# Three transformer-like blocks on one core: the two halves of the tokens are set half a stage apart, each half with its own weight tiles

## The chip, the cores and the metric

One Trainium2 chip; the kernel runs on one of its cores. The metric is the device time of one execution in microseconds (us), the median over runs. A core has TensorE (PE in the rows; its weight loads are PEld), VectorE (DVE), ScalarE (ACT), GpSimd (POOL), and SyncE (SP), which issues all DMAs here. Each of these engines takes its instructions in the one order that the built program gives it.

## The reference, cut to what matters

512 tokens of width 1024 go through three blocks in fp32, ten stages in all, in the order f10, m1, f11, f21, m2, f22, m30, f30, m31, f31:

```
f10, f11   x = x + 0.5*(1+gate) * rms_norm(swiglu(modulate(x)))       # D_FF = 2816
m1         spatial gating on 512 channels beside causal attention with forget gates, then w_out
f21, f22   swiglu with norms before and after
m2         RWKV-7 recurrence (chunks of 64) beside a 31-tap convolution, then w_out_2
m30, m31   attention over the 256 keys that an indexer picks (a), beside differential attention (b)
f30, f31   x = x + swiglu(rms_norm(x))
swiglu(h)  = (silu(h @ w_gate) * (h @ w_up)) @ w_down
```

Each stage needs the stage before it for the same tokens. Half 1 of the tokens also needs keys, values or states of half 0 within a mixer (m1, m2, m30, m31); half 0 needs nothing of half 1.

## The kernel before, in words

The 512 tokens are two halves of 256, `hf` 0 and 1. `for ph in phases: for hf in range(2): part(ph, hf)` writes the program down stage by stage. A scheduler then decides each engine's order: every instruction carries a priority, `BASE + (vt[hf] + lag[hf]) * PER_US`, where `vt` counts the matmul time that this half has had so far (`adv`), and `lag[1]` puts half 1 behind half 0 by a number of such us (`LAGS`, set at each stage's `prenorm`). `boost(us)` makes work more urgent by that much: the chains of the mixers have 20 to 80 us of it, loads of weights mostly none (`WB = 0`).

Weights arrive in fp32, as slots of 128x1024 (eight 128x128 tiles). `Weights.slot` loads a slot into one of three staging buffers (`st`), makes an fp16 high part from it on ScalarE and an fp16 low part on VectorE, and puts both into one of the 12 buffers of a ring (`wr`). `three` multiplies high by high, high by low and low by high, so each tile and half costs three matmuls of 256 columns, and a slot 24 of them. `W(name)` gives the one `Weights` of a matrix, so that a slot is loaded and split once, and both halves read it:

```
def W(name):
    if name not in weights:
        weights[name] = Weights(name)
    return weights[name]
```

In an FFN, `gu` holds 44 slots (22 pairs of gate and up, `pgu` in PSUM, evacuated by `fth`, `fac`, `act`) and `dn` 22 slots (`po`). m1 has 28 slots, m2 30, m30 and m31 35 each; 524 in all. In the mixers, `pp`, `pt` and `pgl` are the projections, `ps` the scores of one head (`amx` their maximum, `prob`, `probt`), `pd` and `sc` the indexer's scores, from which `MAX8` and `MATCH_REPLACE8` pick keys, and `pT`, `pA`, `pxy`, `pu`, `psp` belong to the recurrence of m2. Each half has two PSUM buffers for its scores and two for its projections. While f10 runs, the 37.7 MB of `w_ada` also come in and are summed on VectorE (`ada_row`).

Of the kernel before, what the change touches and what calls it, by code (L numbers as in the profile page):

```python
# [44 lines left out]
RB = 80  # L45
SELB = 5
RING = 12
LAGS = {"f10": 26, "m1": 16, "f11": 22, "f21": 26, "m2": 22, "f22": 24,
    "m30": 30, "f30": 22, "m31": 30, "f31": 18}
HOLD = {"m1": -5, "m2": 15, "m30i": 0, "m30b": -5, "m30a": -5, "m31i": 0,  # L50
    "m31b": 0, "m31a": 0}
BASE = 2000000
# [191 lines left out]
def tile_three_blocks(ctx: ExitStack, tc: tile.TileContext, d, col_at, con_at, out, phases=None):  # L244
# [129 lines left out]

    weights = {}

    def W(name):
        if name not in weights:
            weights[name] = Weights(name)
        return weights[name]  # L380

    def three(out_, a, b, first, last, guard):
        (ah, al), (bh, bl) = a, b
# [126 lines left out]
    def ffn(hf, gu, dn, pre, bias, post, key):  # L510
        hh = prenorm(hf, pre, bias, key)
        acts = []
        for n in range(NF):
            adv(hf, 5.23)
            if n % 2 == 0:
                acts.append(m2k(hf, [128, 2, 2, TH], F16, "act"))
            act = acts[-1]
            p = pmm(hf, [128, 2, TH], name="pgu")
            gemm(p[:, 0], W(gu), 16 * n, KD, pair(hh))
            gemm(p[:, 1], W(gu), 16 * n + 8, KD, pair(hh), bank=False)  # L520
            with boost(EB):
                t = t1k(hf, name="fth")
                S.activation(t, p[:, 0], AF.Tanh, scale=0.5 / WS)  # L523
                V.scalar_tensor_tensor(t, t, 1.0, p[:, 0], op0=OP.add, op1=OP.mult)  # L524
                a = t1k(hf, name="fac")
                V.scalar_tensor_tensor(a, t, 0.5 / WS / WS / AS, p[:, 1], op0=OP.mult, op1=OP.mult)  # L526
                split(hf, act[:, 0, n % 2], act[:, 1, n % 2], a)
            beside(key, hf, n)
        x = lambda k: (acts[k // 2][:, 0, k % 2], acts[k // 2][:, 1, k % 2])
        if post is None:  # L530
            out_add(hf, W(dn), NF, x, AS / WS)
            return
        yb = {}

        def y(m):
            if not yb:
                yb[0] = b8k(hf, [128, KD, TH], F32, "y")
            return yb[0][:, m]
        acc = out_tiles(hf, W(dn), NF, x, y, AS / WS, key)
        postnorm(hf, acc, y, post)  # L540


# [15 lines left out]
    def ada_row(g, k, h):  # L558
        src = kv2k(1, name="adw")
        nc.sync.dma_start(out=src, in_=d["w_ada"][g, k, :, h * 512:(h + 1) * 512])  # L560
        if k == 0:
            ada_acc[g, h] = kv2k(0, name="ada")
            V.tensor_scalar(ada_acc[g, h], src, csil[:, 0:1], None, op0=OP.mult)
        else:
            V.scalar_tensor_tensor(ada_acc[g, h], src, csil[:, k:k + 1], ada_acc[g, h], op0=OP.mult, op1=OP.add)  # L565
# [120 lines left out]
    def mixer1(hf):  # L686
# [24 lines left out]
        for j in range(8):  # L711
            adv(hf, 2.6)
            p = pmm(hf, [128, TH], name="pp")
            gemm(p, W("m1_qk"), (j + 4) % 8 * KD, KD, px)
            with boost(MB):
                (kt if j < 4 else qt_).put(j % 4, p, 1.0 / WS if j < 4 else 0.125 / WS)
        m1["k", hf] = kt
# [28 lines left out]
        m1["v", hf] = []  # L746
        for tt in range(2):
            vt_ = kv2k(hf, name="v")
            token_gemm(hf, W("m1_v"), hh, tt, lambda p: S.activation(vt_, p, AF.Copy, scale=1.0 / WS))
            m1["v", hf].append(vt_)  # L750

        now(hf)
# [24 lines left out]
        for j in range(4):  # L777
            adv(hf, 2.6)
            p = pmm(hf, [128, TH], name="pp")
            gemm(p, W("m1_u"), j * KD, KD, px)  # L780
            if j % 2 == 0:
                us.append(m2k(hf, [128, 2, TH], F32, "u"))
            gelu(hf, us[-1][:, j % 2], p)
# [6 lines left out]
        for tt in range(2):  # L790
            g = m2k(hf, name="vg")

            def ev(p, g=g):
                for q in range(2):
                    gelu(hf, g[:, q * 256:(q + 1) * 256], p[:, q * 256:(q + 1) * 256])
            token_gemm(hf, W("m1_g"), hh, tt, ev)
            bn = tiny(hf, 6, "bn")
            V.bn_stats(bn, g)
            mv = tiny(hf, 2, "mv")
# [31 lines left out]
                to_channels(hf, ybs[qt], mix, 4, qt, lambda j: col("gnb", j))  # L831
        ys = [m2k(hf, [128, 2, TH], F32, "ym") for _ in range(4)]
        y = lambda m: ys[m // 2][:, m % 2]
        acc = out_tiles(hf, W("m1_o"), KD, pair(mix), y, 1.0 / WS)
        postnorm(hf, acc, y, one_col(gpost, 8))

    def row_rms(hf, y, n):
# [20 lines left out]
    def mixer2(hf):  # L858
# [36 lines left out]
        for j in order:  # L895
            adv(hf, 2.6)
            p = pmm(hf, [128, TH], name="pp")
            gemm(p, W("m2_s"), j * KD, KD, px)
            with boost(BOOST["m2r"]):
                raw = t1k(hf, name="raw")  # L900
                S.activation(raw, p, AF.Copy, scale=1.0 / WS)
# [17 lines left out]
        def gate_units(j):  # L919
            adv(hf, 5.2)  # L920
            p = pmm(hf, [128, 2, TH], name="pgl")
            gemm(p[:, 0], W("m2_c"), 16 * j, KD, px)
            gemm(p[:, 1], W("m2_c"), 16 * j + 8, KD, px, bank=False)
# [296 lines left out]
        acc = out_tiles(hf, W("m2_o"), KD, lambda k: (mix[:, k, 0], mix[:, k, 1]), y, 1.0 / WS)  # L1220
        postnorm(hf, acc, y, lambda k: col("mpost2", k))


# [3 lines left out]
    def mixer3(hf, l):  # L1227
# [24 lines left out]
        def rotated(w, i0, dst, tab, scale):  # L1252
            adv(hf, 2.6)
            p = pmm(hf, [128, TH], name="pp")
            gemm(p, W(w), i0 * KD, KD, px)
            with boost(RB):
                sw = t1k(hf, name="rsw")
                for b in range(4):
# [80 lines left out]
        vb = []  # L1339
        for tt in range(2):  # L1340
            t = kv2k(hf, name="vb")
            token_gemm(hf, W(f"m3_vb{l}"), hh, tt, lambda p: S.activation(t, p, AF.Copy, scale=1.0 / WS))
            vb.append(t)
        m3["vb", hf] = vb
        now(hf)
# [43 lines left out]
        with boost(BOOST["m3a"]):  # L1389
# [19 lines left out]
        out_add(hf, W(f"m3_o{l}"), KD, pair(mix), 1.0 / WS)  # L1409

# [88 lines left out]
```

## Time and profile before

| | |
|---|---|
| median of 3 runs | 3501.31 us (3500.28 to 3503.44) |
| the profiled execution | 3507.87 us, its span 3506.0 us |
| PE busy | 3309.1 us, 94% |
| PEld busy | 2815.7 us, 80% |
| DVE busy | 2171.3 us, 62% |
| ACT busy | 1545.5 us, 44% |
| mean granted TensorE clock | 0.98 of full speed |
| bytes | 327.89 MB, mean 94 GB/s |

Busy time is the union of an engine's instructions. A matmul's recorded duration reaches past the start of the next one, so that a PE that waits less than the rest of a matmul still counts as busy. In rows of windows a stretch is given from the start of the span, then its length, and for each engine the busy us and the number of instructions.

### The profile page before, as it was taken

To read this page: it belongs to the slowest core of one execution; us is meant where nothing else is said; L and a number is where in the kernel's file an instruction comes from. 1 tells how busy PE (TensorE), PEld (TensorE's weight loads), DVE (VectorE), ACT (ScalarE), POOL (GpSimd) and SP (SyncE) were. 2 spreads that over 40 slices of the span, in tenths; PEclk is the share of its full clock that TensorE was granted. 3 is DMA by queue.
4 is the path that set the end of the run, shared out by engine and by line. 5 is a ranking of instruction groups with operands and counts; after the bars stand their busy time and mean duration, and the time that the engine had idled before them with its cause. 6 is when DMAs were issued, how large, how long until landed. Compare 5 with 4: busy or idle time off the path is not lost. (4 is left out here: it accounts for less than half of the span.)

```text
span 3506.0 us, 71986 instructions
## 1 busy us (share of the span) xinstructions
PE 3309.1 (94%) x30164; PEld 2815.7 (80%) x30164; DVE 2171.3 (62%) x5240; ACT 1545.5 (44%) x3335; POOL 19.1 (1%) x24
## 2 busy tenths in 40 slices
PE   5999999999999999997789999889999998999998
PEld 5888867788888888886678887667888876688887
DVE  8953768844374437688884438887544488855433
ACT  3332466433343324424243326886433278853331
POOL 0000000000000000000000000000000000000000
PEclk9999999999999999987889999999999999999999
DMA  8932313232323332201023323112233321123331
GB/s 276 326 110 91 118 55 130 67 103 97 99 96 102 104 97 91 70 5 34 4 89 104 102 97 99 55 43 67 85 104 102 105 85 51 41 80 109 103 99 47
DMA packets 105591, 327.89 MB, mean 94 GB/s; under 512 B 12584, under 2 KB 18088, under 8 KB 105008
## 3 DMA queue, kind: packets, MB, share of 16 engines
q1 hardware_dynamic: 105264, 323.28, 28.1%
q8 instruction: 236, 3.87, 0.5%
q14 instruction: 91, 0.75, 0.1%
HBM read 321.14 MB, written 2.10 MB: 92 GB/s over the span
## 5 line engine op out<-in xcount | busy, mean ns | idle before, releaser
L314 PEld LDWEIGHTS <-wr 128*128 128x128 f16 x24000 | 2351.0, 99 | 327.8 <-issue 25.5
L314 PE MATMUL pgu<-hh,wr 128*128 128x256 f16 x12672 | 1402.6, 273 | 7.9 <-ACT wr L362 2.3
L363 DVE SCALAR_TENSOR_TENSOR wr<-st,wr 128x1024 f16<-128x1024 f32 x524 | 640.3, 1223 | 353.3 <-ACT wr L362 344.0
L314 PE MATMUL po<-act,wr 128*128 128x256 f16 x6336 | 702.0, 273 | 0.1
L362 ACT ACTIVATE wr<-st 128x1024 f16<-128x1024 f32 x524 | 552.2, 1055 | 323.2 <-PE pgu L314 128.3
L314 PE MATMUL pp<-hh,wr 128*128 128x256 f16 x3072 | 384.1, 274 | 4.8 <-DVE rot L1261 2.2
L523 ACT ACTIVATE fth<-pgu 128x256 f32<-128x256 f32 x264 | 101.3, 384 | 590.4 <-PE pgu L314 590.2
L524 DVE SCALAR_TENSOR_TENSOR fth<-fth,pgu 128x256 f32<-128x256 f32 x264 | 111.0, 420 | 355.9 <-ACT fth L523 355.8
L314 PE MATMUL po<-mix,wr 128*128 128x256 f16 x1536 | 198.0, 282 | 15.9 <-ACT mix L444 9.0
L444 ACT ACTIVATE act<-fac 128x256 f16<-128x256 f32 x264 | 110.2, 417 | 174.1 <-DVE fac L526 173.8
L314 PE MATMUL pt<-wr,hh 128*128 128x512 f16 x576 | 145.4, 383 | 1.6 <-DVE wr L363 1.6
L445 DVE TENSOR_TENSOR act<-fac,act 128x256 f16<-128x256 f32 x264 | 111.3, 422 | 50.5 <-ACT act L444 50.0
L492 DVE TENSOR_TENSOR acc<-acc,sq 128x256 f32<-128x256 f32 x84 | 35.4, 421 | 149.5 <-ACT sq L491 149.5
L1260 ACT ACTIVATE rsw<-pp 32x256 f32<-32x256 f32 x304 | 114.3, 376 | 19.6 <-PE pp L314 15.3
L432 ACT ACTIVATE sq<-x 128x256 f32<-128x256 f32 x154 | 56.5, 411 | 134.0 <-DVE x L501 129.6
L526 DVE SCALAR_TENSOR_TENSOR fac<-fth,pgu 128x256 f32<-128x256 f32 x264 | 110.8, 420 | 7.7
L485 ACT ACTIVATE y<-po 128x256 f32<-128x256 f32 x64 | 24.5, 383 | 204.8 <-PE po L314 204.7
L941 DVE SCALAR_TENSOR_TENSOR mix<-glu,cols,mix 128x256 f32<-128x256 f32 x240 | 102.2, 477 | 0.1
L314 PEld LDWEIGHTS <-hh 128*128 128x128 f16 x768 | 62.2, 100 | 48.3 <-issue 3.2
L619 DVE TENSOR_REDUCE amx<-ps 128x1 f32<-128x128 f32 (+3 forms) x160 | 77.3, 487 | 34.4 <-PE ps L314 32.6
L565 DVE SCALAR_TENSOR_TENSOR ada<-adw,csil,ada 128x512 f32<-128x512 f32 x126 | 91.0, 747 | 5.8 <-DMA adw<-in_w_ada_dram 5.6
L501 DVE SCALAR_TENSOR_TENSOR x<-po,x 128x256 f32<-128x256 f32 x64 | 26.9, 422 | 108.1 <-PE po L314 108.0
(356 smaller groups left out, 2935.6 us busy)
## 6 DMA issues: line engine op xcount, KB each, us to landing
st<-in_gu_dram SPq DMA_DIRECT2D x264, 512.0 KB, 3.5
st<-in_dn_dram SPq DMA_DIRECT2D x132, 512.0 KB, 3.5
adw<-in_w_ada_dram SPq DMA_DIRECT2D x144, 256.0 KB, 5.2
st<-in_m_o_dram SPq DMA_DIRECT2D x32, 512.0 KB, 3.6
st<-in_m_b_dram SPq DMA_DIRECT2D x16, 512.0 KB, 3.6
st<-in_m_a_dram SPq DMA_DIRECT2D x16, 512.0 KB, 3.8
st<-in_m_s_dram SPq DMA_DIRECT2D x14, 512.0 KB, 3.6
st<-in_m_qk_dram SPq DMA_DIRECT2D x8, 512.0 KB, 4.0
```

Source lines behind the costliest of these rows:

```text
L314: return PE.matmul(out_, lhsT=l, rhs=r, start=start, stop=stop, skip_group_check=True)
L362: S.activation(r[:, 0], st, AF.Copy, scale=WS)
L363: V.scalar_tensor_tensor(r[:, 1], st, WS, r[:, 0], op0=OP.mult, op1=OP.subtract)
L444: S.activation(hi, src, AF.Copy)
L445: V.tensor_tensor(lo, src, hi, op=OP.subtract)
L523: S.activation(t, p[:, 0], AF.Tanh, scale=0.5 / WS)
L524: V.scalar_tensor_tensor(t, t, 1.0, p[:, 0], op0=OP.add, op1=OP.mult)
L526: V.scalar_tensor_tensor(a, t, 0.5 / WS / WS / AS, p[:, 1], op0=OP.mult, op1=OP.mult)
L565: V.scalar_tensor_tensor(ada_acc[g, h], src, csil[:, k:k + 1], ada_acc[g, h], op0=OP.mult, op1=OP.add)
L619: V.tensor_reduce(nm, s[:, :nk], axis=AX.X, op=OP.max, negate=True)
L941: V.scalar_tensor_tensor(cc(j), gl[:, i:i + TH], dw[:, j * 31 + i:j * 31 + i + 1], cc(j), op0=OP.mult, op1=OP.add)
L1260: S.activation(sw[a:a + 32], p[c:c + 32], AF.Copy, scale=scale)
```

## The change

`W` takes the half as well: a matrix has one `Weights` for each half, except `gu10` (named in `TOGETHER`). 480 of the 524 slots are thus loaded and split twice, 1004 in all, and the ring and the staging buffers serve both. The lag of half 1 is 90 in all stages but the first. In f10 it stays 26 in the gate/up part, and `WIDEN` adds 8 at each of the eight output tiles, which makes 90. The last group of the modulation sums is kept in a buffer of the other half.

```diff
-LAGS = {"f10": 26, "m1": 16, "f11": 22, "f21": 26, "m2": 22, "f22": 24,
-    "m30": 30, "f30": 22, "m31": 30, "f31": 18}
+LAGS = {"f10": 26, "m1": 90, "f11": 90, "f21": 90, "m2": 90, "f22": 90,
+    "m30": 90, "f30": 90, "m31": 90, "f31": 90}
+WIDEN = {"f10": 8}
+TOGETHER = ("gu10",)
...
-    def W(name):
-        if name not in weights:
-            weights[name] = Weights(name)
-        return weights[name]
+    def W(name, hf):
+        key = name, hf if name not in TOGETHER else 0
+        if key not in weights:
+            weights[key] = Weights(name)
+        return weights[key]
...
             beside(key, hf, NF + m)
+            if hf and key in WIDEN:
+                lag[1] += WIDEN[key]
             adv(hf, nk * 0.327)
...
-            gemm(p[:, 0], W(gu), 16 * n, KD, pair(hh))
-            gemm(p[:, 1], W(gu), 16 * n + 8, KD, pair(hh), bank=False)
+            gemm(p[:, 0], W(gu, hf), 16 * n, KD, pair(hh))
+            gemm(p[:, 1], W(gu, hf), 16 * n + 8, KD, pair(hh), bank=False)
...
-            ada_acc[g, h] = kv2k(0, name="ada")
+            ada_acc[g, h] = kv2k(g // 8, name="ada")
```

All other uses of `W` change in the same way. Two places of the order follow; a tile's number grows with its place in the written program.

**In f21's gate/up part**, ScalarE before; `pgu_12…` are groups of half 0, `pgu_14…` of half 1. The slot `wr_12963` is for `pgu_12960`:

```order
L523 ACTIVATE fth_12886<-pgu_12827 128x256
L444 ACTIVATE act_12760<-fac_12889 128x256
L362 ACTIVATE wr_12963<-st_12961 128x1024
L523 ACTIVATE fth_14831<-pgu_14782 128x256
L362 ACTIVATE wr_12992<-st_12990 128x1024
L444 ACTIVATE act_14725<-fac_14834 128x256
L523 ACTIVATE fth_12953<-pgu_12894 128x256
```

The same place with the change, ScalarE; all groups are of half 0, and follow each other on TensorE as 12809, 12875, 12942, 13008:

```order
L530 ACTIVATE fth_12868<-pgu_12809 128x256
L366 ACTIVATE wr_12907<-st_12905 128x1024
L449 ACTIVATE act_12808<-fac_12871 128x256
L366 ACTIVATE wr_12945<-st_12943 128x1024
L530 ACTIVATE fth_12934<-pgu_12875 128x256
L366 ACTIVATE wr_12974<-st_12972 128x1024
L449 ACTIVATE act_12808<-fac_12937 128x256
L366 ACTIVATE wr_13011<-st_13009 128x1024
```

And TensorE with the change, the middle of the group `pgu_12942`, where it goes over to its second slot:

```order
L316 LDWEIGHTS wr_12945
L316 MATMUL pgu_12942<-hh_12775,wr_12945 128x256
L316 LDWEIGHTS wr_12974
L316 MATMUL pgu_12942<-hh_12775,wr_12974 128x256
L316 LDWEIGHTS wr_12974
```

Before, three other groups stand between the evacuation ahead of a split and the group that needs this split. With the change, `wr_12974` is split behind the evacuation of `pgu_12875`, and the group that comes right after 12875, `pgu_12942`, needs it in its middle.

**In m30, while half 1 is at its projections and scores**, VectorE before; `rsa_26911` and `drs_26910` are of half 0, numbers of 28000 on of half 1:

```order
L655 TENSOR_TENSOR hl_28414<-rot_28610,hd_28412 64x256
L407 SCALAR_TENSOR_TENSOR rsa_26911<-drs_26910,dss_26780 128x4
L1317 MATCH_REPLACE sc_28178<-m8_28250,sc_28178 128x384
L408 TENSOR_TENSOR rsa_26911<-rsa_26911,drs_26910 128x4
L1316 MAX m8_28253<-sc_28178 128x8
L1261 SCALAR_TENSOR_TENSOR rot_28690<-pp_28691,rope64_28005 128x256
L1262 TENSOR_TENSOR rsw_28716<-rsw_28716,rope64_28005 128x256
L409 SCALAR_TENSOR_TENSOR drs_26910<-rsa_26911,drs_26910 128x4
```

The same place with the change, VectorE; all tiles are of half 1:

```order
L1324 MATCH_REPLACE sc_29583<-m8_29667,sc_29583 128x384
L662 TENSOR_TENSOR hl_29819<-rot_30130,hd_29818 64x256
L1323 MAX m8_29670<-sc_29583 128x8
L633 RECIPROCAL ars_30300<-asm_30298 128x1
L662 TENSOR_TENSOR hl_29820<-rot_30130,hd_29818 64x256
L1324 MATCH_REPLACE sc_29583<-m8_29670,sc_29583 128x384
L367 SCALAR_TENSOR_TENSOR wr_30785<-st_30783,wr_30785 128x1024
L626 TENSOR_REDUCE amx_30308<-ps_30302 128x1
L1323 MAX m8_29673<-sc_29583 128x8
```

Before, the two halves' chains alternate here, row by row. With the change half 0 has left the mixer, and half 1's second copies of the mixer's weights (`wr_30785`) stand between the rows of its own chain.

## Rows read from the trace of the kernel before

**Rows 1.** The page: PE's busy line, then busy tenths in 40 slices, GB/s.
```profile
PE 3309.1 (94%) x30164; PEld 2815.7 (80%) x30164; DVE 2171.3 (62%) x5240; ACT 1545.5 (44%) x3335; POOL 19.1 (1%) x24
...
PE   5999999999999999997789999889999998999998
...
DVE  8953768844374437688884438887544488855433
...
PEclk9999999999999999987889999999999999999999
...
GB/s 276 326 110 91 118 55 130 67 103 97 99 96 102 104 97 91 70 5 34 4 89 104 102 97 99 55 43 67 85 104 102 105 85 51 41 80 109 103 99 47
```

**Rows 2.** Windows by stage: f10; m1; m2; f22; m30; m31 (last columns PEclk, DMA, GB/s).
```profile
88.00:351.00 263.00, 262.94 (x2410) 236.12 (x2408) 157.03 (x271) 81.88 (x140) 0.00 (x0) 1.00 0.52 175
351.00:701.00 350.00, 332.57 (x2715) 262.59 (x2714) 258.31 (x746) 188.77 (x443) 3.78 (x4) 0.99 0.28 93
...
1315.00:1841.00 526.00, 470.71 (x5267) 390.62 (x5266) 411.53 (x1224) 209.01 (x473) 0.00 (x0) 0.91 0.15 49
1841.00:2104.00 263.00, 263.00 (x2412) 235.74 (x2410) 107.97 (x169) 85.88 (x143) 0.00 (x0) 1.00 0.31 101
2104.00:2542.00 438.00, 400.31 (x3312) 316.98 (x3311) 337.79 (x917) 295.87 (x747) 7.57 (x8) 0.98 0.22 70
...
2805.00:3243.00 438.00, 406.42 (x3438) 326.69 (x3436) 324.44 (x845) 294.24 (x733) 5.68 (x6) 1.00 0.23 73
```

**Rows 3.** Windows: half 1's first projection to the next FFN, in m1, m2, m30, m31.
```profile
447.00:659.00 212.00, 202.01 (x1555) 149.73 (x1554) 156.24 (x478) 129.09 (x319) 0.00 (x0) 0.98 0.29 94
...
1396.00:1801.00 405.00, 355.76 (x4253) 290.38 (x4252) 319.55 (x954) 156.05 (x359) 0.00 (x0) 0.88 0.13 40
2194.00:2453.00 259.00, 232.15 (x1793) 171.63 (x1793) 212.58 (x603) 206.08 (x551) 1.89 (x2) 0.97 0.17 56
2870.00:3132.00 262.00, 236.12 (x1870) 177.73 (x1869) 216.59 (x604) 206.91 (x552) 1.89 (x2) 0.99 0.19 58
```

**Rows 4.** Groups by line: count, busy us, mean ns, idle before and its releasers.
```profile
L314 PE MATMUL pgu<-hh,wr 128*128 128x256 f16 x12672 | 1402.6, 273 | 7.9 <-ACT wr L362 2.3 <-ACT hh L444 1.6 <-ACT hh L441 1.4
...
L363 DVE SCALAR_TENSOR_TENSOR wr<-st,wr 128x1024 f16<-128x1024 f32 x524 | 640.3, 1223 | 353.3 <-ACT wr L362 344.0 <-issue 0.3
L362 ACT ACTIVATE wr<-st 128x1024 f16<-128x1024 f32 x524 | 552.2, 1055 | 323.2 <-PE pgu L314 128.3 <-PE po L314 121.5 <-DMA st<-in_gu_dram 35.1
```

**Rows 5.** The same view, VectorE's largest groups in m30 (512-column forms).
```profile
L1261 DVE SCALAR_TENSOR_TENSOR rot<-pp,rope 128x256 f32<-128x256 f32 x76 | 32.2, 423 | 28.9 <-ACT rsw L1260 27.8
L619 DVE TENSOR_REDUCE amx<-ps 128x1 f32<-128x512 f32 x40 | 27.5, 686 | 10.1 <-PE ps L314 9.5
...
L1316 DVE MAX8 m<-sc 128x8 f32<-128x512 f32 x32 | 21.8, 682 | 0.1
L1317 DVE MATCH_REPLACE8 sc<-m,sc 128x512 f32<-128x512 f32 x32 | 21.6, 676 | 0.0
```

**Rows 6.** Timeline in f21: start us, length us, engine, operation.
```profile
1147.54 0.39 ACT L523 ACTIVATE fth<-pgu 128x256 f32<-128x256 f32 x1 [1.62 <-PE pgu L314]
1147.82 1.05 ACT L362 ACTIVATE wr<-st 128x1024 f16<-128x1024 f32 x1
1147.95 0.42 DVE L524 SCALAR_TENSOR_TENSOR fth<-fth,pgu 128x256 f32<-128x256 f32 x1 [0.78 <-ACT fth L523]
1148.41 0.42 DVE L526 SCALAR_TENSOR_TENSOR fac<-fth,pgu 128x256 f32<-128x256 f32 x1
...
1148.90 1.23 DVE L363 SCALAR_TENSOR_TENSOR wr<-st,wr 128x1024 f16<-128x1024 f32 x1
```

**Rows 7.** DMA issues: queue, count, KB each, median us to landing.
```profile
st<-in_gu_dram SPq DMA_DIRECT2D x264, 512.0 KB, 3.5
```

**Rows 8.** SP's issue of weight loads: ns min/median/max of one.
```profile
L360 SPq DMA_DIRECT2D st<-in_gu_dram x264: 327/328/1278, 28.8 to 3316.8; - x132
```

**Rows 9.** Window of line 363 alone: DVE busy (count), clock, DMA share, GB/s.
```profile
3067.00:3076.00 9.00, 5.14 (x5) 1.00 0.65 213
```

More of the change, by code (lines that the diff above doesn't have):

```diff
@@ L530, in ffn @@
         if post is None:
-            out_add(hf, W(dn), NF, x, AS / WS)
+            out_add(hf, W(dn, hf), NF, x, AS / WS)
             return
@@ L538, in y @@
             return yb[0][:, m]
-        acc = out_tiles(hf, W(dn), NF, x, y, AS / WS, key)
+        acc = out_tiles(hf, W(dn, hf), NF, x, y, AS / WS, key)
         postnorm(hf, acc, y, post)
@@ L713, in mixer1 @@
             p = pmm(hf, [128, TH], name="pp")
-            gemm(p, W("m1_qk"), (j + 4) % 8 * KD, KD, px)
+            gemm(p, W("m1_qk", hf), (j + 4) % 8 * KD, KD, px)
             with boost(MB):
@@ L748, in mixer1 @@
             vt_ = kv2k(hf, name="v")
-            token_gemm(hf, W("m1_v"), hh, tt, lambda p: S.activation(vt_, p, AF.Copy, scale=1.0 / WS))
+            token_gemm(hf, W("m1_v", hf), hh, tt, lambda p: S.activation(vt_, p, AF.Copy, scale=1.0 / WS))
             m1["v", hf].append(vt_)
@@ L779, in mixer1 @@
             p = pmm(hf, [128, TH], name="pp")
-            gemm(p, W("m1_u"), j * KD, KD, px)
+            gemm(p, W("m1_u", hf), j * KD, KD, px)
             if j % 2 == 0:
@@ L795, in ev @@
                     gelu(hf, g[:, q * 256:(q + 1) * 256], p[:, q * 256:(q + 1) * 256])
-            token_gemm(hf, W("m1_g"), hh, tt, ev)
+            token_gemm(hf, W("m1_g", hf), hh, tt, ev)
             bn = tiny(hf, 6, "bn")
@@ L833, in mixer1 @@
         y = lambda m: ys[m // 2][:, m % 2]
-        acc = out_tiles(hf, W("m1_o"), KD, pair(mix), y, 1.0 / WS)
+        acc = out_tiles(hf, W("m1_o", hf), KD, pair(mix), y, 1.0 / WS)
         postnorm(hf, acc, y, one_col(gpost, 8))
@@ L897, in mixer2 @@
             p = pmm(hf, [128, TH], name="pp")
-            gemm(p, W("m2_s"), j * KD, KD, px)
+            gemm(p, W("m2_s", hf), j * KD, KD, px)
             with boost(BOOST["m2r"]):
@@ L921, in gate_units @@
             p = pmm(hf, [128, 2, TH], name="pgl")
-            gemm(p[:, 0], W("m2_c"), 16 * j, KD, px)
-            gemm(p[:, 1], W("m2_c"), 16 * j + 8, KD, px, bank=False)
+            gemm(p[:, 0], W("m2_c", hf), 16 * j, KD, px)
+            gemm(p[:, 1], W("m2_c", hf), 16 * j + 8, KD, px, bank=False)
             with boost(GB):
@@ L1219, in mixer2 @@
         y = lambda m: ys[m // 2][:, m % 2]
-        acc = out_tiles(hf, W("m2_o"), KD, lambda k: (mix[:, k, 0], mix[:, k, 1]), y, 1.0 / WS)
+        acc = out_tiles(hf, W("m2_o", hf), KD, lambda k: (mix[:, k, 0], mix[:, k, 1]), y, 1.0 / WS)
         postnorm(hf, acc, y, lambda k: col("mpost2", k))
@@ L1254, in rotated @@
             p = pmm(hf, [128, TH], name="pp")
-            gemm(p, W(w), i0 * KD, KD, px)
+            gemm(p, W(w, hf), i0 * KD, KD, px)
             with boost(RB):
@@ L1341, in mixer3 @@
             t = kv2k(hf, name="vb")
-            token_gemm(hf, W(f"m3_vb{l}"), hh, tt, lambda p: S.activation(t, p, AF.Copy, scale=1.0 / WS))
+            token_gemm(hf, W(f"m3_vb{l}", hf), hh, tt, lambda p: S.activation(t, p, AF.Copy, scale=1.0 / WS))
             vb.append(t)
@@ L1383, in mixer3 @@
             t = kv2k(hf, name="va")
-            token_gemm(hf, W(f"m3_va{l}"), hh, tt, lambda p: S.activation(t, p, AF.Copy, scale=1.0 / WS))
+            token_gemm(hf, W(f"m3_va{l}", hf), hh, tt, lambda p: S.activation(t, p, AF.Copy, scale=1.0 / WS))
             va.append(t)
@@ L1408, in mixer3 @@
                 to_channels(hf, yas[qt], mix, 0, qt, None)
-        out_add(hf, W(f"m3_o{l}"), KD, pair(mix), 1.0 / WS)
+        out_add(hf, W(f"m3_o{l}", hf), KD, pair(mix), 1.0 / WS)
     def finish(hf):
```

## The prediction

> **What bounds the kernel now.** I read the page first [rows 1]: TensorE is busy 94% of the span, and in the FFN stretches its slices are full while VectorE's stand at 3 to 8 tenths. The windows by stage [rows 2] say the same with numbers: f22 has PE busy 263.0 of 263 us beside 108 us of VectorE, f10 262.9 of 263. The idle time sits in the mixers: m1 17 us (350 - 333), m2 55, m30 38, m31 32, together 142; the rest of the 197 us is nearly all at the start and the end. PE's busy time hides short waits, because a matmul lasts 273 ns in the records and takes 0.111 us when they follow closely (1402.6 us for 12672) [rows 4]. So I also counted PE's work in the order, each matmul at its closest spacing (0.11 us for 256 columns of fp16, the other kinds by their own), and set it beside the time. For that I use the same stretch in each mixer, from half 1's first projection to the first gate/up group of the next FFN [rows 3]: m1 185 us of PE work in 212 us, m2 309 in 405, m30 196 in 259, m31 215 in 262. That is 27 + 96 + 63 + 47 = 233 us lost, and VectorE is busy there for 74, 79, 82 and 83% of the time. Add up the durations of VectorE's rows in these stretches (174, 379, 233, 242 us) and the time was 1.22, 1.07, 1.11 and 1.08 us for each of them. Durations overlap by some 0.08 us when rows follow closely, so a VectorE that never pauses would need about 0.9 us. In m30 ScalarE is just as full, 206 of 259 us.
>
> **What the change adds.** 480 slots more are loaded and split. At 1.223 us each on VectorE and 1.055 us on ScalarE [rows 4] that is 587 and 506 us: VectorE goes from 2171 to some 2760 us, ScalarE from 1546 to some 2050. SP issues 480 loads more at 0.33 us [rows 8], 157 us in which nothing else waits that is not a weight or a small table. The bytes go from 328 to 580 MB, 165 GB/s on average; an FFN takes a slot per 2.66 us (24 matmuls at 0.111) instead of 5.3, which is 197 GB/s. The second slice already moved 326 GB/s [rows 1] with PE full, so I cost the bytes at nothing; a load lands in 3.5 us [rows 7], and five splits in 9 us [rows 9] is 1.8 us for each, faster than 2.66. In FFN stretches VectorE has room: f22 would have 108 us plus 50 more splits, 61 us, of 263. What is left over for these splits is hidden there; without that room it would be the whole 587.
>
> **Weights that come just in time, +10 us.** In the FFN stretches with a single half, the order shows the second slot of a group split behind the evacuation of the group before it. 64 slots in the order stand so that less than one slot's work lies between that evacuation's group and their first use; before, 5 do within even 3.2 us. Their chain is in the timeline [rows 6]: the tanh starts at 1147.54, the low part would be done at 1148.90 + 1.23 = 1150.13, 2.59 us later. The tanh can start 0.16 us (273 - 111 ns) and a hand-over (0.03 us between ScalarE's split and VectorE's, to perhaps 0.1) after the next group's start, so the low part is there at 2.8 to 2.85. The third matmul of the slot wants it at 26 x 0.111 less a weight load of 0.09 (2815.7 us for 30164) [rows 1], 2.79. A stall of 0 to 0.3 us each, with what a release costs; I take 0.15, 64 x 0.15 = 10 us, bounds 0 and 19.
>
> **The mixers, +81 us.** Does the other half's FFN really cover a mixer? The order says: only in part. In m30, PE's rows from half 1's first projection to the next `pgu` are 907 instead of 1596: 456 projections, 96 of `pt` and the scores, almost all of half 1, 108 us of work. Beside it VectorE has 331 rows: 27 splits (33 us), 32 MAX8 and 32 MATCH_REPLACE8 (20 and 19 us), 24 maxima (14 us), 57 of the rotation (24 us), by the means of their groups [rows 4, 5], and small ones; 165 us together. Where 233 us of VectorE stood beside 196 of PE (1.19), 165 stand beside 108 (1.53). The FFN work of the other half comes before (29 us of f22's output) and behind (89 us of f30).
>
> I cut each mixer into three: half 0 up to half 1's first projection; on to the next `pgu`; on to half 1's last matmul. PE work and VectorE durations, in us: m1 94 and 107, 104 and 112, 124 and 108. m2 173 and 207, 77 and 96, 206 and 229. m30 142 and 165, 108 and 165, 129 and 93. m31 122 and 137, 128 and 183, 129 and 93. The time of a piece is the larger of PE's work and VectorE's durations times a factor. Measured factors are 1.07 to 1.22 [rows 3]; the added splits wait for no matmul and fill pauses, which speaks for less; one half's chains alone, with two score buffers in flight instead of four, speak for more. I take 1.07, the lowest measured. The loss beyond PE's work is then 36 us in m1 (20 + 16 + 0), 113 in m2 (48 + 26 + 39), 103 in m30 (35 + 69 + 0), 92 in m31 (25 + 68 + 0): 345 us. Before, it was 233 us in the middles, and 31 us for the first and last pieces at the same factor, 264. Net +81. What is late next is PE's `ps` and `pp`, as their PSUM buffers come free later.
>
> Bounds: at a factor of 1.00 the mixers lose 247 us, net -17; at 1.14, in the middle of the measured ones, 443 us, net +179.
>
> The TensorE clock: in m2's middle 0.88 of full speed was granted [rows 3], so part of it ran at 1.2 instead of 2.4 GHz, after stretches in which PE waited. The Trainium skill, "TensorE: Matmul & The Clock Gate", Part 1, says that the low clock is the default and that activity lifts it; by that rule f21's and f22's matmuls beside m2 would hold it up. No more than 0.12 x 356 = 43 us are there to win, and while VectorE sets the pace there a faster PE only waits longer, so the sum has nothing for it; the faster rival has.
>
> Start and end stay: the order on PE is the same for the first 2264 matmuls, and the end still is half 1's output, its norm and store. The moved modulation sums are as many as before. Sum: 81 + 10 = +91. The profiled execution took 3507.87 us, 6.6 over the median of 3501.31; its span is 3506.0, so the sum gives a span near 3597, and on the median 3592.
>
> **Rivals.** *The mixers are covered after all, about 3400 us.* If splits and chains of both halves let VectorE run with hardly a pause, the factor is 0.93 (97% busy where 0.9 is a VectorE without any), the mixers lose 149 us, net -115, with the 10 us -105: 3396. For it: f10's second slice, with VectorE at 9 tenths and PE full. Against it: there the work was `w_ada` sums that wait for nothing but DMA, and no mixer stretch got VectorE above 83%. It decides at a factor of 1.01, about 89% VectorE in the middles; below that the change wins.
>
> *No change, 3494 to 3508.* The factor is 1.0, the coverage pays for the splits: -17 + 10 gives 3494. For it: idle ScalarE and VectorE in all FFN pieces. Against: the middles of m30 and m31, where at any factor over 0.8 VectorE sets the pace.
>
> *The FFNs starve, about 3680 us.* Three staging buffers serve twice the slots. If a load, its two splits and their waits take 8.4 instead of 8.0 us (3 x 2.66), each of the 616 slots of f10's output and the other FFNs costs 0.14 us, 86 us on top: 3678. For it: 3.5 + 1.06 + 1.22 us is 5.8 before any wait, and in-order queues add waits. Against: 1.8 us per split in a mixer [rows 9].
>
> **How the numbers follow.** Chances: the forecast with its own bounds (3520 to 3650) 0.53; the covered mixers 0.15; no change 0.12; starving FFNs 0.20. The likeliest gives 3592. The range runs from 3480, inside the faster rival, to 3690, just past the starving one and the upper factor, and leaves out about 2 in 10. About 0.2%, 7 us, is what a measurement of this kernel can tell from no change: faster 0.17, same 0.08, slower 0.75; the upper part of "no change" reaches into slower.
>
> **What would show it.** Right: PE at full busy in FFN stretches except for short waits for the split's line; in m30 and m31 a middle piece of 110 to 130 us of PE work that takes 170 to 200 us, with VectorE at 82 to 88%; idle PE in the mixers up from 142 to some 190 us or more. Wrong to the fast side: PE over 95% busy throughout m30. Wrong to the slow side: ScalarE's split waiting for DMA, or PE waiting for line 367 all through the FFNs.

## The result, and the profile after

The changed kernel takes 3706.82 us (median of 4 runs, 3703.36 to 3720.45) against 3502.38 us: a ratio of 1.0583, 95% interval 1.0547 to 1.0620. It is slower, as forecast, but by 204 us instead of 91, and 17 us past the upper end of the range. The profiled execution took 3708.09 us, its span is 3706.2 us.

The page of the changed kernel: busy lines, then busy tenths in 40 slices, clock and GB/s, as in [rows 1].

```profile
PE 3373.0 (91%) x30155; PEld 2839.4 (77%) x30164; DVE 2719.6 (73%) x5720; ACT 2014.4 (54%) x3815; POOL 19.1 (1%) x24
...
PE   6999978999999999979989988888999988789998
...
DVE  8955777786767676987877678787666787967664
...
PEclk9999989999999999979989999888999999989999
...
GB/s 276 310 109 188 172 104 141 178 167 202 177 194 182 196 178 173 8 125 172 61 83 178 208 162 125 125 52 138 161 191 210 179 103 154 41 129 190 191 207 116
```

VectorE's and ScalarE's busy time grew by 548 and 469 us (587 and 506 were worked out from durations, which overlap). TensorE's busy time has grown by 64 us although its matmuls are the same; the rest of the 200 us in the span is idle time. Where it lies, the windows tell: first the three pieces of m1, m2, m30 and m31 into which the prediction cut the mixers (half 0 up to half 1's first projection, on to the next `pgu`, on to half 1's last matmul), then the FFN stretches after each of them (columns as in [rows 2]).

```profile
394.00:526.00 132.00, 106.04 (x790) 79.51 (x789) 95.73 (x266) 78.27 (x174) 1.89 (x2) 0.90 0.42 132
526.00:660.00 134.00, 115.72 (x874) 86.87 (x873) 99.56 (x237) 84.95 (x186) 0.00 (x0) 0.95 0.39 130
660.00:792.00 132.00, 129.17 (x1171) 112.21 (x1172) 106.11 (x216) 75.30 (x128) 0.00 (x0) 1.00 0.61 188
1405.00:1616.00 211.00, 182.34 (x2282) 151.39 (x2281) 175.87 (x490) 91.44 (x185) 0.00 (x0) 0.93 0.26 86
1616.00:1713.00 97.00, 85.76 (x696) 70.60 (x693) 81.05 (x207) 60.53 (x122) 0.00 (x0) 0.92 0.47 145
1713.00:1964.00 251.00, 233.05 (x2648) 192.84 (x2649) 202.77 (x510) 112.08 (x218) 0.00 (x0) 0.93 0.33 104
2207.00:2398.00 191.00, 164.97 (x1271) 124.63 (x1272) 147.99 (x388) 146.55 (x367) 2.83 (x3) 0.94 0.38 124
2398.00:2567.00 169.00, 134.05 (x964) 99.80 (x962) 148.58 (x366) 123.42 (x291) 1.89 (x2) 0.85 0.26 82
2567.00:2703.00 136.00, 134.41 (x1170) 117.72 (x1175) 88.58 (x137) 76.96 (x133) 0.00 (x0) 0.97 0.53 173
2941.00:3102.00 161.00, 137.50 (x1085) 103.02 (x1084) 125.53 (x325) 129.36 (x327) 2.83 (x3) 0.97 0.42 134
3102.00:3297.00 195.00, 155.09 (x1146) 117.50 (x1145) 163.96 (x397) 137.46 (x318) 1.89 (x2) 0.87 0.26 83
3297.00:3431.00 134.00, 133.19 (x1172) 116.98 (x1176) 89.39 (x137) 77.01 (x134) 0.00 (x0) 0.98 0.54 176
...
792.00:1405.00 613.00, 584.81 (x5250) 513.16 (x5248) 417.45 (x701) 311.49 (x474) 0.00 (x0) 0.99 0.58 186
1964.00:2207.00 243.00, 227.09 (x2027) 198.75 (x2025) 164.96 (x285) 122.05 (x189) 2.84 (x3) 0.99 0.57 185
2703.00:2941.00 238.00, 234.26 (x2118) 206.95 (x2115) 161.99 (x257) 119.96 (x171) 2.84 (x3) 0.99 0.62 197
3431.00:3706.00 275.00, 262.01 (x2376) 231.93 (x2373) 168.12 (x274) 118.74 (x166) 0.00 (x0) 0.98 0.53 171
```

TensorE idles 232 us in the twelve pieces of the mixers, and 61 us in the four FFN stretches. The same cut of the kernel before (mixers 413:666, 1365:1809, 2150:2501, 2804:3167; FFNs 666:1365, 1809:2150, 2501:2804, 3167:3506) has 128 and 30 us, by the sums of these windows:

```profile
sum 1411.00, PE 1283.35 PEld 1009.82 DVE 1106.38 ACT 846.85 POOL 10.40; mean PE 320.84 PEld 252.45 DVE 276.60 ACT 211.71 POOL 2.60
...
sum 1682.00, PE 1652.00 PEld 1472.44 DVE 794.38 ACT 558.70 POOL 4.73; mean PE 413.00 PEld 368.11 DVE 198.60 ACT 139.67 POOL 1.18
```

So 104 us of the loss is idle time in mixers, 31 in FFNs, and 64 is busy time that got longer. The clock column stands at 0.85 and 0.87 in the middle pieces of m30 and m31, where [rows 3] had 0.97 and 0.99: a part of their matmuls ran at 1.2 instead of 2.4 GHz.

What TensorE waited for in the changed kernel (us in total, times, longest):

```profile
PE nbc L316 <- DVE ndg L426: 39.1, 29, 7.7
PE nst L316 <- DVE acc L438: 30.2, 15, 8.6
...
PE pgu L316 <- DVE fac L533: 21.2, 10, 2.9
PE pch L1198 <- DVE yt L1193: 20.1, 3, 9.2
...
PE pgu L316 <- ACT wr L366: 7.6, 4, 2.8
...
PE po L316 <- DVE fac L533: 5.6, 2, 2.9
...
PE pgu L316 <- DVE wr L367: 2.4, 4, 1.0
```

The waits of gate/up for a split sum to 10.0 us, the amount forecast. New are 27 us in which `pgu` and `po` wait for `fac`, the last evacuation of an earlier group; in the kernel before these waits sum to 1.0 us. The timeline of VectorE at the end of a stage shows how they arise (start, length, operation):

```profile
974.12 0.15 DVE L421 TENSOR_SCALAR nm<-nst 128x2 f32<-128x2 f32 x1
...
974.59 1.21 DVE L367 SCALAR_TENSOR_TENSOR wr<-st,wr 128x1024 f16<-128x1024 f32 x1
975.73 0.16 DVE L410 TENSOR_SCALAR ny<-ny 128x2 int32<-128x2 int32 x1
975.90 0.42 DVE L531 SCALAR_TENSOR_TENSOR fth<-fth,pgu 128x256 f32<-128x256 f32 x1
976.24 0.15 DVE L412 SCALAR_TENSOR_TENSOR rsa<-ny,nm 128x2 f32<-128x2 f32 x1
976.31 1.22 DVE L367 SCALAR_TENSOR_TENSOR wr<-st,wr 128x1024 f16<-128x1024 f32 x1
...
978.86 1.23 DVE L367 SCALAR_TENSOR_TENSOR wr<-st,wr 128x1024 f16<-128x1024 f32 x1
...
981.45 1.23 DVE L367 SCALAR_TENSOR_TENSOR wr<-st,wr 128x1024 f16<-128x1024 f32 x1 [0.89 <-ACT wr L366]
982.59 0.48 DVE L426 TENSOR_SCALAR ndg<-ident,ny 128x128 f32<-128x128 f32 x2
```

The norm's chain from `nm` to `ndg` is twelve rows of 0.15 us or so. Here it takes 8.47 us, with four splits and four rows of the other half's gate/up among its links; where nothing stands between, it takes 2.4 us in both kernels. Splits among the links are not new: in the kernel before, a chain at a stage end takes up to 6.7 us with three of them, and `nbc` waits 1.5 to 2.0 us for it. New is what comes behind it: TensorE's `nbc` stands in its row and waits, then the eight `nh` and eight `hh` rows of the norm hold up `fac`, and `pgu` waits too. With a first wait for `fac`, behind the rows of the norm before, this makes gaps of some 2.1, 1.8 and 3.2 us, one behind the other, at each of five stage ends.

### The profile page after: what moved, and what is told of

The parts are those of the page before. It is cut to its first block, busy times and chain, and to the rows that moved or that the text cites. A ratio compares the mean times of both kernels' runs of the same rounds, so it can differ in the third digit from the quotient of the medians.

```text
span 3706.2 us, 74678 instructions
## 1 busy us (share of the span) xinstructions
PE 3373.0 (91%) x30155; PEld 2839.4 (77%) x30164; DVE 2719.6 (73%) x5720; ACT 2014.4 (54%) x3815; POOL 19.1 (1%) x24
## 4 chain that ended last, share of the span: by engine, by line
PE 65%; DVE 14%; ACT 12%; DMA 5%; issue 3%; SPq 0%; ACTq 0%; DVEq 0%
PE pgu L316 31%; PE po L316 18%; ACT wr L366 4%; PE pp L316 4%; DVE wr L367 4%; PE ps L316 3%; ACT rsw L1267 3%; PE pT L316 2%; DMA st<-in_gu_dram 1%; DMA st<-in_dn_dram 1%; PE ps L638 1%; PE pt L316 1%; ACT hd L661 1%; PE pxy L316 1%; DVE acc L438 1%
## 5 line engine op out<-in xcount | busy, mean ns | idle before, releaser
L367 DVE SCALAR_TENSOR_TENSOR wr<-st,wr 128x1024 f16<-128x1024 f32 x1004 | 1225.4, 1223 | 515.8 <-ACT wr L366 501.8
L316 PE MATMUL pgu<-hh,wr 128*128 128x256 f16 x12672 | 1441.8, 275 | 32.7 <-DVE fac L533 21.2
L366 ACT ACTIVATE wr<-st 128x1024 f16<-128x1024 f32 x1004 | 1054.9, 1054 | 613.1 <-PE pgu L316 208.6
L316 PE MATMUL po<-act,wr 128*128 128x256 f16 x6336 | 725.8, 273 | 5.6 <-DVE fac L533 5.6
L316 PE MATMUL pp<-hh,wr 128*128 128x256 f16 x3072 | 395.6, 283 | 27.5 <-DVE hd L665 9.0
L316 PE MATMUL po<-mix,wr 128*128 128x256 f16 x1536 | 180.3, 276 | 5.4 <-ACT mix L449 4.2
L316 PE MATMUL ps<-hd 128*128 128x256 f16 (+1 forms) x240 | 62.5, 274 | 41.5 <-ACT prob L631 17.5
L631 ACT ACTIVATE prob<-ps,amx 128x128 f32<-128x128 f32 (+3 forms) x160 | 83.7, 523 | 25.5 <-DVE amx L626 21.4
L640 ACT ACTIVATE probt<-ps 128x256 f32<-128x256 f32 (+3 forms) x128 | 55.7, 435 | 57.6 <-PE ps L638 55.8
```

The source lines that it names most:

```text
L316: return PE.matmul(out_, lhsT=l, rhs=r, start=start, stop=stop, skip_group_check=True)
L366: S.activation(r[:, 0], st, AF.Copy, scale=WS)
L367: V.scalar_tensor_tensor(r[:, 1], st, WS, r[:, 0], op0=OP.mult, op1=OP.subtract)
L631: S.activation(p[:, :nk], s[:, :nk], AF.Exp, bias=nm, scale=scale, accum_out=sm)
```

## The experiments

Eighteen kernels were run, each beside the kernel before (3500.5 to 3503.1 us). Where a kernel leaves work out, its expectation says which part.

**The two halves of the change apart.** One run has the copies at the old lags, one the shared slots at a longer lag, one the copies at a still longer lag.

```diff
 # copies_only: two copies, lags and WIDEN of the kernel before
+LAGS = {"f10": 26, "m1": 16, "f11": 22, "f21": 26, "m2": 22, "f22": 24,
+    "m30": 30, "f30": 22, "m31": 30, "f31": 18}
+WIDEN = {}
 # lag45_shared: all names in TOGETHER, lag 45 ("f10": 26, and 8 x 2.5)
 # lag108: the changed kernel with 108 for 90, and 8 x 10.25 in f10
```

> Each half has its own copies (1004 splits), but the lags are those of the kernel before (16 to 30 us). Theory LAG (the loss comes from where the halves stand: one half's chains alone in the mixers, and norms that fall beside the other half's gate/up): the halves alternate in the mixers as before, the extra splits fill pauses of VectorE, 3500 to 3560. Theory SPLITS (the 587 us more of VectorE are the loss): 3650 or more. Between them, by the prediction's own rule (VectorE's durations in the mixers' middles, with 28 to 35 more splits of 1.223 us each, times 1.07): 223, 445, 285 and 298 us instead of 212, 405, 259 and 262, so +113, about 3615.

Measured: 3675.5 us, ratio 1.0505 (1.0474 to 1.0537), inside the range of SPLITS and 60 us above the prediction's own rule. With the old lags the copies cost 173 us. LAG is refuted in its strong form: the longer lag adds only 31 us to the copies.

> Every matrix shared by the halves again (524 splits), lag 45 in all stages. LAG: half of the way to 90, norms of half 1 fall 45 us into half 0's gate/up (about 11 us for each of some 4 boundaries instead of 5) and the mixers' chains alternate over a shorter stretch: 3540 to 3600. SPLITS: no split is added, 3500 to 3515. A third thing can add to it: a slot now stays in the ring of 12 for 45 us and more, and a lag beyond what the ring holds (12 slots at 5.3 us are 64 us) would show as TensorE waiting for the split's lines.

Measured: 3657.2 us, ratio 1.0446 (1.0424 to 1.0469). Not what either theory said. My bound for the ring was wrong: a lag of 45 us of one half's matmul time is some 90 us of the clock while both halves work, and 12 slots at 5.3 us are 64. ScalarE waited 437 us in front of a split for `pgu` or `po` to give a slot back (215.4 and 221.4), against 250 before (128.3 and 121.5). Below, the same lag without a shared ring is faster than before; so this run is about the ring.

> As the changed kernel, with a lag of 108 instead of 90. LAG, its part on norms: half 1's norms now fall beside half 0's output part (88 to 131 us of an FFN), half 0's some 23 us into half 1's gate/up, as before the change; of the 80 us lost in the FFN windows (41 in f11 and f21, 22 in f22, 18 in f30 and f31) 25 to 35 come back: 3670 to 3685, if the mixers stay as they are (within 20 us). SPLITS: no change, 3700 to 3710.

Measured: 3687.9 us, ratio 1.0545 (1.0513 to 1.0577). 19 us came back, less than LAG's 25 to 35 and more than SPLITS' none. Without copies (below) the same step gives 6 us, too little to tell from none; that the rest hangs on the splits in the norms' chains is likely, but not shown.

**VectorE's share.** Half 1's low parts are written as zeros by GpSimd, at lag 90 and at the old lags.

```diff
-V.scalar_tensor_tensor(r[:, 1], st, WS, r[:, 0], op0=OP.mult, op1=OP.subtract)
+if self.second:          # the Weights of half 1, outside gu10
+    G.memset(r[:, 1], 0.0)
+else:
+    V.scalar_tensor_tensor(r[:, 1], st, WS, r[:, 0], op0=OP.mult, op1=OP.subtract)
 # free_copies: G.memset(r, 0.0), and no S.activation, for half 1
```

> As the changed kernel at lag 90, but the low part of half 1's copies is not computed: GpSimd, which is idle, writes zeros there (part of the computation is left out; TensorE's work, the loads and ScalarE's splits stay). 480 splits of 1.223 us leave VectorE. SPLITS: back to 3500 or below. LAG in its pure form (the chain of one half alone is paced by latency, not by how full VectorE is): 3680 to 3700. By the prediction's rule (durations times 1.07 in the mixers, some 15 splits less in each of the first and last pieces and some 30 in the middles of m2, m30 and m31, and fewer splits inside the norms' chains): about 180 to 220 less, 3490 to 3530.

Measured: 3589.3 us, ratio 1.0248 (1.0206 to 1.0290): 117 us less. None of the three ranges held it. The splits on VectorE are over half of the loss, not all.

> As the run with copies at the old lags (3675.5 us), but the low part of half 1's copies is not computed (GpSimd writes zeros; part of the computation is left out): 480 splits of 1.223 us leave VectorE, while the loads and ScalarE's splits stay doubled. Theory ROW (what copies cost is VectorE's row, where the extra splits stand between the links of the chains): 3500 to 3550, nearly all of the 173 us back. Rival LOADS (what costs are 480 more loads through three staging buffers and ScalarE's splits, with which everything behind them on ScalarE waits): 3600 or more.

Measured: 3577.6 us, ratio 1.0213 (1.0180 to 1.0247): 98 us less than with both copies at the old lags, and 74 more than before. Neither range held it: the splits on VectorE are the larger part, and something else costs 74 us.

> As the changed kernel at lag 90, but half 1's copies are zeros written by GpSimd, both parts (part of the computation is left out): no second split on ScalarE or VectorE; the loads are issued still, and nothing reads them. What is left is the lag of 90 by itself. ROW: the zeros of the low part alone gave 3589, and ScalarE's splits add little: 3565 to 3595, so the lag by itself costs 65 to 95 us. LOADS: 3500 to 3540, and the lag by itself costs next to nothing.

Measured: 3585.7 us, ratio 1.0229 (1.0199 to 1.0260), inside ROW's range and 4 us under the run before. I took this for the price of ScalarE's second splits. But GpSimd now writes 128x2048 where it wrote 128x1024, and while it does so some rows of VectorE are held up:

```profile
953.33 1.86 DVE L414 TENSOR_SCALAR ny<-ny 128x2 int32<-128x2 int32 x1
953.36 1.80 POOL L368 MEMSET wr<- 128x2048 f16 x1 [2.12 <-PE pgu L316]
```

Such a link of a norm's chain takes 0.17 us by itself. The durations of VectorE's rows sum to 2450 us in this run, 2418 with zeros for the low part alone and 2412 with the fixed slot below, and TensorE's `nbc` waits 50 us for `ndg` where it waits 34 in those two. So up to some 32 us of GpSimd's doing stand in this time, and ScalarE's second splits may cost up to that much more than 4 us. I also read the 83 us that were left as the price of the lag; the fixed slot shows that this was wrong.

**Blocking or sum.** Every low part in two instructions of half the length.

```diff
+for a in range(0, 1024, 512):
+    V.scalar_tensor_tensor(r[:, 1, a:a + 512], st[:, a:a + 512], WS, r[:, 0, a:a + 512], op0=OP.mult, op1=OP.subtract)
```

> The changed kernel with every low part made by two instructions of 512 columns instead of one of 1024. A link of a chain then waits for at most 0.6 to 0.75 us of a split instead of 1.22, while VectorE's sum grows (512-column rows take 0.69 us, so 1004 x 0.15 = 150 us over the whole kernel, some 40 of it in the mixers). If the splits cost by blocking (a link waits for the split ahead of it): 3630 to 3690. If they cost by VectorE's sum: 3720 to 3750. LOADS: 3700 to 3715.

Measured: 3750.0 us, ratio 1.0703 (1.0665 to 1.0740). The group of the halved splits on VectorE:

```profile
L368 DVE SCALAR_TENSOR_TENSOR wr<-st,wr 128x512 f16<-128x512 f32 x2008 | 1332.5, 687 | 502.8 <-ACT wr L366 488.6
```

2008 rows of 687 ns are 1380 us instead of 1004 x 1.223 = 1228, and the kernel is 43 us slower. VectorE's sum costs; a shorter block in front of a link gains nothing that outweighs it.

**A version that might have been faster.** The kernel before, with GpSimd making the low parts of the mixers' 128 slots.

```diff
+if self.name[0] == "m":
+    G.tensor_scalar(st, st, WS, None, op0=OP.mult)
+    G.tensor_tensor(r[:, 1], st, r[:, 0], op=OP.subtract)
```

> The kernel before (shared weights, old lags), but the low parts of the mixers' 128 slots are made by GpSimd in two instructions (times 64 in place, minus the high part) and not by VectorE: 157 us leave VectorE's row where it sets the pace. ROW: by the prediction's rule 30 to 40 us each in m2, m30 and m31 at most, 3400 to 3470, if GpSimd's two instructions together stay under some 5 us (a slot is wanted every 5.3 us) and don't slow VectorE. LOADS, or if VectorE's sum doesn't matter: 3495 to 3510. If GpSimd takes longer than 5.3 us for a slot, or holds up VectorE, slower than before: 3520 to 3700, with TensorE waiting for GpSimd's line.

Measured: 3743.6 us, ratio 1.0683 (1.0655 to 1.0711). Two rows of GpSimd, what TensorE waited for it, and a group of VectorE, all of this kernel:

```profile
L364 POOL TENSOR_SCALAR st<-st 128x1024 f32<-128x1024 f32 x128 | 365.9, 2859 | 2242.7 <-ACT wr L362 2113.0 <-issue 47.4 <-PE ps L314 36.5
L365 POOL TENSOR_TENSOR wr<-st,wr 128x1024 f16<-128x1024 f32 x128 | 279.0, 2180 | 10.2
...
PE pp L314 <- POOL wr L365: 24.1, 11, 3.4
PE pt L314 <- POOL wr L365: 22.5, 10, 4.1
PE po L314 <- POOL wr L365: 16.8, 6, 3.7
...
L480 DVE TENSOR_TENSOR x<-x,nh 128x256 f32<-128x256 f32 x96 | 56.8, 620 | 0.1
```

A slot takes GpSimd 5.04 us, TensorE waits 63 us for it, and VectorE's rows with two inputs got longer: `x<-x,nh` 620 instead of 420 ns. It is 44 us slower even than the range given for a GpSimd that holds things up. So the run says little on ROW.

**The lag without copies.** Half 1 multiplies by one slot that is in place from the start.

```diff
+fixed = cons.tile([128, 2, 1024], F16, name="fixed")
+V.memset(fixed, 0.0)
...
 def slot(self, s):
+    if self.second:
+        return fixed
```

> Half 1 has no copies to make at all: outside of f10's gate/up it multiplies by one fixed slot that is in place from the start (its loads and splits are left out, the rest of the work stays), the ring has 11 slots, lags of the kernel before. Theory SUM (copies cost by the time that their splits take on VectorE and ScalarE): no copies, so 3490 to 3510, and the 75 us that remained with zeros for the low part were ScalarE's second splits. Rival ORDER (the halves no longer share a slot, so the scheduler sets them differently, whatever the copies cost): 3550 to 3580.

Measured: 3511.9 us, ratio 1.0030 (1.0009 to 1.0051), 2 us above SUM's range. ORDER is out.

> As the run with the fixed slot for half 1, lag 45. It tells what the lag costs without copies and without a ring that holds a slot for both halves. If the lag by itself costs: half of what it costs at 90, 3530 to 3560. If the 3657 of the shared slots at lag 45 were the lag and not the ring: 3630 or more. Theory SUM says nothing on the lag but that it is paid on top: at most the cost at 90.

Measured: 3473.7 us, ratio 0.9929 (0.9904 to 0.9955). I had expected a cost; the lag by itself gains 28 us.

> The changed kernel at lag 90 with the fixed slot for half 1: the lag by itself. SUM with a lag that costs: 3560 to 3590, as with zeros (3589 and 3586). If those were high because GpSimd's writes held up VectorE (its rows were 32 us longer in the second of them) or because of ScalarE's splits: 3500 to 3550.

Measured: 3485.5 us, ratio 0.9963 (0.9937 to 0.9989), below both ranges. By itself the lag of the change gains 16 us over the kernel before and 26 over the fixed slot at the old lags. All of the 204 us, and 16 more, are the copies'.

> As the run with the fixed slot, lag 108. With copies 108 was 19 us faster than 90; if that came from the norms of half 1 now beside half 0's output part, it is there without copies too: 10 to 20 us under the run at 90. If it came from where the copies' splits fall: the same as at 90, within 8 us.

Measured: 3479.3 us, ratio 0.9946 (0.9917 to 0.9976), 6 us under the run at 90, inside the range of "the same, within 8 us"; the two intervals overlap.

**One cost at a time, added to the fixed slot at lag 90.**

```diff
 if self.second:
+    if s not in self.have:
+        self.have[s] = fixed
+        # add_dve (add_act: S.activation(spare, zeros, ...); add_loads: st and its dma_start)
+        V.scalar_tensor_tensor(spare, zeros, WS, fixed[:, 0], op0=OP.mult, op1=OP.subtract)
     return fixed
 # ring6: RING = 6 instead of 11, nothing added
```

> The kernel with the fixed slot at lag 90 (3485.5), and one instruction on VectorE of a split's shape (from the fixed slot to a spare tile, 1.2 us) for each slot that half 1 no longer makes: 480 of them, 587 us, which wait for nothing. Ring of 10. SUM: the 117 us that left with these splits come back, 3590 to 3620. If the splits cost by their waits (for the load, ScalarE's part and the ring) and not by VectorE's time: 3490 to 3520.

Measured: 3553.7 us, ratio 1.0162 (1.0144 to 1.0180). Where the 480 added rows ran (the tile `spare` in this run: count and times of start, then busy tenths in 40 slices):

```profile
L366 DVE SCALAR_TENSOR_TENSOR spare<-fixed x480: 1189/1218/1227, 3.6 to 1308.1; 128x1024 f16<-128x1024 f32 x160
...
busy tenths in 40 slices 1055622344747450000000000000000000000000
```

All of them ran in the first 1310 us: the scheduler takes a row that waits for nothing as soon as its engine is free. They stood in f10, m1, f11 and f21, none in m2, m30 or m31. The time lies between the two ranges. Even so, a VectorE that was 9 tenths busy for 1200 us cost 68 us.

> The same on ScalarE: 480 instructions of a split's shape, 1.05 us each, 506 us, which wait for nothing. Ring of 10. If ScalarE's time is the open part: 3560 to 3590. If it fills ScalarE's pauses: 3485 to 3510; in m30 and m31, where ScalarE is 80% busy, some 10 us each are likely, so about 3505.

Measured: 3520.0 us, ratio 1.0071 (1.0044 to 1.0098), between the ranges; its rows ran before 840 us. The 34 us are too early in the program to say what copies cost.

> The same kernel with half 1's 480 loads into the three staging buffers, which nobody reads. If bytes, the issue on SP or the staging buffers are the open part: 3550 to 3590. If they are hidden: 3480 to 3500.

Measured: 3601.9 us, ratio 1.0304 (1.0283 to 1.0326), above both ranges. Not usable either: the added loads seem to have run ahead in bursts, with real loads behind them. Six gaps of TensorE of 8 to 23 us, 85 us together, make up most of it; three are waits of a projection or of gate/up for a slot, as long as 15.2 us, and with real copies such a wait is at most 2.8 us.

> The same kernel with a ring of 6 slots instead of 11: half 0's slots are made no further ahead than when half 1's copies fill the other half of 12. If the depth of the ring is the open part (splits that can't be made ahead stand in the mixers' rows): 3550 to 3590. If not: 3480 to 3505.

Measured: 3518.3 us, ratio 1.0056 (1.0041 to 1.0071). Between the ranges: a ring of half the depth costs 33 us, a third of what was open.

**One cost at a time, taken out.**

```diff
 # free_noload: free_copies without st and its dma_start for half 1
 # no_loads: the changed kernel, half 1's slots split from a constant
+st = ident[:, None, :].to_broadcast([128, 8, 128])
```

> As the run with zeros for half 1's copies (both parts written by GpSimd, 3586), and half 1's 480 loads left out too. What then remains over the fixed slot (3486) is that half 1's copies take ring slots, and GpSimd's writes. If the loads are the open 100 us: 3485 to 3510. If the shared ring is: 3570 to 3590.

Measured: 3588.1 us, ratio 1.0241 (1.0208 to 1.0274), inside the range given for the shared ring.

> The changed kernel, ring and both splits of every slot kept, but half 1's copies are split from a constant that is in place, not from loaded weights (their 480 loads are left out, so half 1 multiplies by other numbers). If the loads cost some 100 us: 3600 to 3630. If they are hidden and the splits' place in the rows is what costs: 3690 to 3710.

Measured: 3652.0 us, ratio 1.0433 (1.0400 to 1.0466): 55 us less than the changed kernel, between the two ranges.

Put in a row at lag 90, each run with one thing more for half 1: fixed slot 3485.5; slots of the shared ring, filled with zeros 3588.1; their loads too 3585.7; ScalarE's splits too 3589.3; VectorE's splits too 3706.8. The two steps that count are the ring, 103 us, and VectorE's splits, 118 us. In the second and third of these runs up to some 32 us are GpSimd's, as said above; in the fourth, where VectorE's rows are only 6 us longer than with the fixed slot, the ring, the loads and ScalarE's splits cost 104 us together. By these numbers, as an estimate, the ring by itself costs some 70 to 100 us and ScalarE's second splits up to 30; no run parts them more finely. Loads cost nothing where nobody waits for them, and 55 us where both splits do.

What the shared ring changes shows in where the halves stand. The indexer's small product `piw` is made once for each half of a layer. In m30 half 0's and half 1's stand 260 us apart with the fixed slot:

```profile
2077.60 1.35 PE L316 MATMUL piw<-swm_w,hh 128*128 128x8 f16 x48 [0.59 <-DVE rot L1273]
...
2337.98 1.35 PE L316 MATMUL piw<-swm_w,hh 128*128 128x8 f16 x48
```

and 187 us with zeros in the shared ring and no loads, at the same lag of 90:

```profile
2190.59 1.35 PE L316 MATMUL piw<-swm_w,hh 128*128 128x8 f16 x48
...
2377.23 1.35 PE L316 MATMUL piw<-swm_w,hh 128*128 128x8 f16 x48
```

It is 191 us in the changed kernel. With the ring of 6 for half 0 alone half 1's first projection in m30 follows half 0's by 256 us, as with the fixed slot. So the shared ring draws the halves together, which depth alone does not do. The stretch in which both halves are in FFNs, from half 1's last output projection of m2 to half 0's first of m30, grows from 159 us with the fixed slot to 252: FFN work that no longer lies beside a mixer.

## Why the prediction was right in its sign and wrong in its size

**Bytes and FFN stretches at nothing.** Half right. `pgu` waited 10.0 us for splits, as in the term for weights just in time (10). But the loads were not free: 55 us went with them. I had priced that as the rival of starving FFNs, at 86 us, by a TensorE that waits for weights. It came in another way, by the sign that I had named: ScalarE waits 123 us at an FFN split for its load (74.8 and 48.2 in two groups, against 35.1 before), and what stands behind that split waits along, so that the norms and the evacuations come late. Without the loads `nst` waits 16.2 instead of 30.2 us for `acc`, and `pgu` 12.4 instead of 21.2 for `fac`.

**The mixers' pieces.** By the rule (the larger of PE's work and VectorE's durations times 1.07) the twelve pieces take 1881 us; they took 1943, 62 more. The middle pieces of m2, m30 and m31 were as forecast or shorter (103 by the rule against 97 measured, 177 against 169, 196 against 195), with VectorE busy for 84, 88 and 84%. m2's first was shorter too, 221 against 211, and the last ones took 5 to 8 more. The step that failed is "I take 1.07, the lowest measured", for m1's first two pieces, 114 against 132 and 120 against 134, and the first ones of m30, 177 against 191, and m31, 147 against 161. The factors there are 1.16 to 1.23, and VectorE is busy for only 73 to 78%: VectorE's sum does not set the time there. In m1's first piece both halves are in a chain at once (half 1's norm after f10, half 0's way to its output); the longest wait of `nst`, 8.6 us, stands there.

**No term for the stage ends in the FFN stretches.** The 10 us for weights just in time were all that I had there, and the second step that failed. The idle time doubled, from 30 to 61 us, and the waits for `fac` make up 26 of these 31. I had looked for splits that come late, and not for a norm whose rows and splits hold up the other half's evacuations. Counted as time for each matmul, these stretches took 0.1118 us before (1682 us for 15043) and 0.1163 now (1369 for 11771), which is 53 us more, 43 over the term. With the 62 of the pieces that is 105 of the 109 us by which the profile's 200 exceed the sum of 91. These stretches say where the time went, and the experiments what it came from; no run joins the two piece by piece.

**The cause was misplaced.** The forecast leaned on the halves no longer alternating ("one half's chains alone, with two score buffers in flight instead of four, speak for more"). The fixed slot shows the opposite: at lag 90 and without copies the kernel is 16 us faster than before. What I left out is that two sets of copies share one ring of 12 slots. By the estimate above it costs some 70 to 100 us at lag 90, of which a ring of half the depth accounts for 33. The rest goes with halves that stand closer than with the fixed slot at the same lag, 187 us instead of 260 in m30. That one half's FFN for this reason doesn't last until the other half's chains need it is argued from these distances; a ring of twice the depth, which would show it, was not tried, since the memory is full.

**The rivals.** Covered mixers and no change are refuted by the range of the ratio. VectorE as the one that sets the pace is right for 118 us: that much goes when its second splits go, and 43 us come when its splits take 150 us longer.

**The clock.** The sum had nothing for it. In m2's middle the granted clock rose, from 0.88 in [rows 3] to 0.92, as the prediction had supposed that f21's and f22's matmuls would do; in the middles of m30 and m31 it fell to 0.85 and 0.87, and the mean from 0.98 to 0.96. No run separates its share.

## What to carry to other kernels

Before a kernel trades shared buffers for a freer order, count what the copies share: a ring that two users fill holds half as much work for each, and it ties them to each other, so that the freedom that was bought is bounded by it. An added row on an engine that is 62% busy is not free if it lands between the links of a chain: cost it where the scheduler puts it, norms and stage ends included. To measure one cost by adding it, make the added work wait for what the real work waits for; otherwise the scheduler runs it early, where it tells nothing. To measure one by leaving it out, look at what stands in for it: GpSimd's zeros cost time of their own.

## What was not expected of the hardware

GpSimd's two-input and in-place rows over 128x1024 fp32 took 2.18 and 2.86 us, and while it worked VectorE's TENSOR_TENSOR rows got longer: `x<-x,nh` from 420 to 620 ns on the mean of all 96, 1024 ns for the 24 that ran wholly beside these rows of GpSimd and 418 ns for the 68 that ran clear of them. Rows `nh<-x,cols,nbc`, whose last input is in PSUM, took 474 and 475 ns. When GpSimd only wrote zeros, the same row took 416 ns. The Trainium skill, "SBUF — State Buffer", section "Who interferes with whom", says that a VectorE instruction with two SBUF inputs contends with a GpSimd instruction that reads SBUF, and not with one that only writes it; these rows agree with both halves of that. A row with one tile as input was held up by zeros all the same: in the run with both parts zeros TENSOR_SCALAR `ny<-ny` over 128x2 took 1.86 us beside a memset of 1.80 us, and 0.17 us by itself.
